# Down-projections of a two-layer decoder trunk: seven pairs of chunks by seven products in place of eight

## The chip, the cores and the metric

The kernel runs on one core of one Trainium2 chip, in one launch. The time is the device time of an execution in microseconds (us). The engines are PE (matmuls; PEld is its loading of the stationary operand), DVE, ACT, POOL, and SP, which here issues nearly all transfers (DMA). Tiles live in SBUF, and matmul results in PSUM, which has eight banks of 128 x 512 fp32.

## What is computed

The reference is a trunk of two layers over a stream of 512 tokens with 1024 features. Layer 0 has dilated window attention, layer 1 forgetting attention, and each is followed by a gated feed-forward network (FFN) with a causal convolution of width 3. The change is in that network, whose hidden width is 2816:

```python
def conv_ffn(xn, w_up, cw, cb, w_down):
    a = xn @ w_up
    ...
    a = sum(ap[:, j:j + T] * cw[j] for j in range(CONV_W)) + cb
    gate, val = jnp.split(a, 2, axis=-1)
    return (jax.nn.gelu(gate, approximate=True) * val) @ w_down
...
    f = conv_ffn(rms_norm(h, g[2]), w_up[l], conv_w[l], conv_b[l], w_down[l])
    h = h + rms_norm(f, g[3])
```

So the down-projection is a product of 512 x 2816 hidden values with a weight of 2816 x 1024, once in each layer.

## The kernel before, in words

**Precision.** Every fp32 operand is split into a high part (a cast to fp32r on ACT) and a low part (the rest, a subtraction on DVE). A product is three matmuls into one bank, high by high, high by low and low by high: `mm3`, lines 236 to 238.

**Weights.** The class `Weights` (line 25 on) holds the list of all weight pieces, 128 x 1024 fp32 or 0.5 MB each, in the order of their use. `load` issues their transfers on SP (line 41), a few pieces ahead; `high` casts a piece on ACT (line 49) and `low` makes the low part on DVE (line 55); `get` hands out the next piece, and `take` gives raw pieces to code that does its own splitting. Raw pieces live in the pool `p4` (9 buffers of 4 KB a partition), split ones in `p8` (17 buffers of 8 KB). A new tile waits for the last use of the tile whose buffer it gets.

**Order.** The program is written out by hand in Python; every engine runs its own instructions in that order, and so does SP with its transfers. A wait on one instruction holds up all that stands behind it on the same engine.

**The FFN** (`ffn`). The hidden width is cut into 22 chunks of 128. For each chunk c, PE multiplies two weight pieces (gate and value) with the transposed input into two banks of 128 features x 512 tokens; ACT and DVE apply the convolution (`taps`, lines 535 to 538), ACT the GELU (line 554), DVE the product of both (line 551), and the result goes to DRAM (`hD`). The chunks in `SEVEN` (6, 8, ..., 20) are done as 2 x 2 blocks in Strassen's way (Winograd's form): seven products of half size (256 wide) in place of eight, with sums of weights made on DVE (`seven_weights`) and sums of the input made once (`sums_in`). While chunk c runs, the steps of `weights(c + 2)` are worked off between its products.

**The down-projection** (`Proj`). For each of the 22 chunks, the hidden values come back from `hD` two chunks at a time (`load_h`, line 516, tile hraw), are split (`prep`, lines 523 and 524, tile hs), and are the stationary operand, 128 tokens at a time; the weight piece (128 x 1024) is the moving one, in two halves of 512. The four token blocks by two halves take all eight banks (`acc`), each being added to over all chunks. A chunk is 4 x 2 x 3 = 24 matmuls. The first 18 chunks run chunk by chunk; the last four (R = 4) run bank by bank, so that each finished bank can be normed and added to the stream while PE goes on. In chunks 20 and 21 of the up-projections the first two hidden tiles and the first weights of the down-projection are prepared already (`load_h(0)`, `prep(0)`, `prep(1)`, `plain_weights`).

## Time and profile before

| what | value |
|---|---|
| median of 3 runs | 1158.45 us (1158.24 to 1158.78) |
| the profiled execution | 1158.71 us |
| its span, first to last instruction | 1156.9 us |
| mean granted clock of PE | 0.999 |
| PE, DVE, ACT, POOL busy | 99%, 66%, 48%, 11% of the span |
| moved by DMA | 138.90 MB, 120 GB/s in the mean |
| down-projection of layer 0, on PE | from 419.08 us on |

A row of the order of time has start, duration, engine, line, operation, output<-input and shape, then in brackets the idle time before it and what ended that. A row of a group has the count, then busy time and mean duration in ns, then the idle time before such instructions and what ended it. A row of busy time by stretch has the stretch, its length, busy time and number of instructions of PE, PEld, DVE, ACT and POOL, the granted clock, the share of the DMA engines and GB/s. Matmuls are pipelined: the distance of two starts is what one costs, and the duration is longer than that.

### The profile page before, as it was taken

What the parts mean: (1) busy time and instruction counts of PE and PEld (TensorE: products, weight loads), DVE (VectorE), ACT (ScalarE), POOL (GpSimd) and SP (SyncE); (2) the same over time, 40 slices, a digit from 0 to 9 for tenths busy, and PEclk for the clock granted to TensorE, in tenths of its full rate; (3) what the DMA queues carried; (4) which work ended last, traced back from release to release, by engine and by line L of the source; (5) the groups of instructions that cost most, each with busy time, mean ns of one, the idle gap of its engine ahead of it and who ended that gap; (6) DMA issues with size and microseconds to landing.
All of it is one profiled execution on the core that took longest, in us unless ns stands there. A gap on an engine that the chain in (4) does not pass through costs nothing.

```text
span 1156.9 us, 16648 instructions
## 1 busy us (share of the span) xinstructions
PE 1142.1 (99%) x6474; PEld 977.5 (84%) x6474; DVE 767.1 (66%) x1227; ACT 554.9 (48%) x956; POOL 131.5 (11%) x191
## 2 busy tenths in 40 slices
PE   9999999999999999999999999999999999999997
PEld 6888889888998888888778888789888998888886
DVE  6433488888878766306564788758788888867204
ACT  5444565444445545305452677755454444445202
POOL 2722003000000000000000565502100000000000
PEclk9999999999999999999999999999999999999999
DMA  8131064334344449203304344274334434539001
GB/s 295 56 111 37 2 173 123 101 110 143 112 127 140 154 158 375 75 1 78 89 1 129 101 118 126 77 203 128 101 92 129 145 105 143 169 124 379 1 1 73
DMA packets 147176, 138.90 MB, mean 120 GB/s; under 512 B 6809, under 2 KB 120969, under 8 KB 147098
## 3 DMA queue, kind: packets, MB, share of 16 engines
q1 hardware_dynamic: 145818, 133.64, 36.7%
q0 software_dynamic: 1280, 4.20, 1.6%
q8 instruction: 51, 0.84, 0.3%
q14 instruction: 27, 0.22, 0.1%
HBM read 119.94 MB, written 13.68 MB: 116 GB/s over the span
## 4 chain that ended last, share of the span: by engine, by line
PE 90%; DVE 4%; ACT 3%; issue 2%; DVEq 0%; ACTq 0%
PE up L236 12%; PE up L237 12%; PE up L238 12%; PE acc L236 9%; PE acc L238 9%; PE acc L237 9%; PE v_ps L236 2%; PE v_ps L238 2%; PE v_ps L237 2%; PE qk_ps L237 2%; PE qk_ps L236 2%; PE qk_ps L238 2%; PE first L238 1%; PE first L236 1%; PE first L237 1%
## 5 line engine op out<-in xcount | busy, mean ns | idle before, releaser
L55 DVE TENSOR_TENSOR w<-wraw,w 128x1024 fp32r<-128x1024 f32 x150 | 189.6, 1279 | 119.2 <-ACT w L49 117.4
L49 ACT CAST w<-wraw 128x1024 fp32r<-128x1024 f32 x150 | 154.2, 1049 | 81.4 <-PE acc L238 56.0
L236 PE MATMUL acc<-w,hs 128*128 128x512 f32 (+1 forms) x356 | 137.9, 387 | 1.1 <-DVE mix L283 1.1
L238 PE MATMUL acc<-w,hs 128*128 128x512 f32 (+1 forms) x356 | 137.6, 387 | 0.0
L237 PE MATMUL acc<-w,hs 128*128 128x512 f32 (+1 forms) x356 | 137.6, 387 | 0.0
L535 ACT ACTIVATE bb<-up,conv 128x512 f32<-128x512 f32 x80 | 60.4, 775 | 149.3 <-DVE up L686 90.9
L236 PE MATMUL up<-xch,w 128*128 128x512 f32 (+1 forms) x288 | 102.2, 355 | 1.7 <-DVE csum L671 1.7
L236 PE MATMUL up<-xbh,w 128*128 128x512 f32 (+1 forms) x288 | 102.1, 355 | 1.7 <-DVE csum L671 1.7
L237 PE MATMUL up<-xcl,w 128*128 128x512 f32 (+1 forms) x288 | 102.0, 354 | 0.0
L237 PE MATMUL up<-xbl,w 128*128 128x512 f32 (+1 forms) x288 | 102.0, 354 | 0.0
L238 PE MATMUL up<-xch,w 128*128 128x512 f32 (+1 forms) x288 | 101.8, 354 | 0.0
L238 PE MATMUL up<-xbh,w 128*128 128x512 f32 (+1 forms) x288 | 101.8, 354 | 0.0
L236 PEld LDWEIGHTS acc<-w,hs 128*128 128x128 f32 x356 | 66.8, 188 | 14.8 <-DVE mix L283 1.3
L237 PEld LDWEIGHTS acc<-w,hs 128*128 128x128 f32 x356 | 66.8, 188 | 13.6
L238 PEld LDWEIGHTS acc<-w,hs 128*128 128x128 f32 x356 | 66.8, 188 | 13.5
L236 PE MATMUL up<-xsh,w 128*128 128x256 f32 x256 | 72.4, 283 | 0.0
L237 PE MATMUL up<-xsl,w 128*128 128x256 f32 x256 | 72.4, 283 | 0.0
L238 PE MATMUL up<-xsh,w 128*128 128x256 f32 x256 | 72.4, 283 | 0.0
L536 DVE SCALAR_TENSOR_TENSOR bb<-up,conv,bb 128x511 f32<-128x511 f32 x80 | 59.4, 743 | 7.2 <-ACT bb L535 7.2
L276 ACT ACTIVATE junk<-acc 128x512 bf16<-128x512 f32 (+1 forms) x33 | 19.2, 582 | 92.4 <-PE acc L238 92.1
L236 PEld LDWEIGHTS up<-xbh,w 128*128 128x128 f32 x288 | 54.4, 189 | 9.5 <-ACT w L49 1.8
L236 PEld LDWEIGHTS up<-xch,w 128*128 128x128 f32 x288 | 54.4, 189 | 9.5 <-ACT w L49 1.8
(273 smaller groups left out, 2662.4 us busy)
## 6 DMA issues: line engine op xcount, KB each, us to landing
wraw<-in_w_up_dram SPq DMA_DIRECT2D x88, 512.0 KB
wraw<-in_w_down_dram SPq DMA_DIRECT2D x44, 512.0 KB
hD<-hc SPq DMA_DIRECT2D x44, 256.0 KB
hraw<-hD SPq DMA_DIRECT2D x22, 512.0 KB
wraw<-in_w_kvf_dram SPq DMA_DIRECT2D x16, 512.0 KB
wraw<-in_w_qkv_a_dram SPq DMA_DIRECT2D x16, 256.0 KB
wraw<-in_w_q_b_dram SPq DMA_DIRECT2D x8, 512.0 KB
ck<-cd SPq DMA_DIRECT2D x8, 512.0 KB
```

What stands on the lines that cost most here:

```text
L49: self.nc.scalar.copy(pair[:, 0], raw)
L55: self.nc.vector.tensor_tensor(pair[:, 1], raw, pair[:, 0].bitcast(F32), ALU.subtract)
L236: pe.matmul(o, ah, bh, start=first, stop=False, skip_group_check=shared)
L237: pe.matmul(o, ah, bl, start=False, stop=False, skip_group_check=shared)
L238: pe.matmul(o, al, bh, start=False, stop=last, skip_group_check=shared)
L276: act.activation(junk[:, :s.stop - s.start], o, AF.Square, scale=1.0 / 32, accum_out=ss[:, n % 2:n % 2 + 1])
L535: act.activation(bb[:, s, :], ps, AF.Identity, bias=cp[:, 3, ch:ch + 1], scale=cp[:, 2, ch:ch + 1])
L536: dve.scalar_tensor_tensor(bb[:, s, 1:], ps[:, :T - 1], cp[:, 1, ch:ch + 1], bb[:, s, 1:], ALU.mult, ALU.add)
```

## The change

Chunks 0 to 13 of the down-projection become seven pairs. A pair is a 2 x 2 block product: the halves of the tokens (256 each) by its two chunks, times its two chunks by the halves of the output (512 each). It is done with seven products of halves and sums in place of eight. The seven pairs are added up product by product, so the sums that belong to the outputs have to be undone in the banks only once, for all pairs together.

- First pass: for each pair, `pair_one` makes sums and differences of the two weight pieces and of the two hidden chunks and splits three tiles; `mul_one` runs four of the seven products, into four banks for each of two block pairs bp (token blocks bp and bp + 2).
- `combine_one`: four additions on DVE and two copies on ACT turn the four banks of a block pair, in place, into the starts of the four outputs.
- Second pass: for each pair, `pair_two` takes the second chunk's weights again (loaded a second time), and the remaining operands, and `mul_two` runs the other three products, added straight into the banks.
- The order of the weight pieces follows: 0 to 13, then 1, 3, ..., 13 again, then 14 to 21.
- Chunks 14 to 21 run in `Proj` as before, which now begins at chunk 14 with the banks that it is given.
- `SEVEN` ends at 18, so chunk 20 of the up-projection is done with whole products. During chunks 20 and 21 `pair_one(0)` and `pair_one(1)` are worked off, in place of the splitting of whole weights and of `prep`.

```diff
+SEVEN = range(6, 19, 2)
+ND = 7
...
-        add_rows(w_down[l], NF)
+        add_rows(w_down[l], [*range(2 * ND), *range(1, 2 * ND, 2), *range(2 * ND, NF)])
...
-        def __init__(self, KC, R, get_act):
+        def __init__(self, KC, R, get_act, begin=0, banks=None):
...
-    SEVEN = range(6, NF - 1, 2)
...
         def weights(c):
+            if c >= NF:
+                return pair_one(c - NF)
             return seven_weights(c) if c in SEVEN else plain_weights()
+        acts, keep, one, two = {}, {}, {}, {}
+        Q = [slice(i * 256, i * 256 + 256) for i in range(4)]
+        H = slice(0, 512), slice(512, 1024)
+
+        def pair_load(j):
+            if j < ND:
+                acts[j] = t8([128, 2, 1024], name="dact")[:, 0]
+                keep[j] = t8([128, 2, 1024], name="dkeep")
+                sp.dma_start(acts[j][:, H[0]], hD[2 * j])
+                sp.dma_start(keep[j][:, 0, H[0]], hD[2 * j + 1])
+
+        def pair_one(j):
+            pair_load(j + 1)
+            r0, r1 = W.take(2)
+            a, k, t = acts.pop(j), keep[j][:, 0], keep[j][:, 1]
+            wa, wb, ac = (t8([128, 2, 1024], F32R, name="w") for _ in range(3))
+            dve.tensor_tensor(t[:, H[1]], r1[:, H[1]], r0[:, H[1]], ALU.subtract)
+            dve.tensor_tensor(r0[:, H[1]], r0[:, H[1]], r0[:, H[0]], ALU.subtract)
+            act.copy(wa[:, 0], r0)
+            yield
+            dve.tensor_tensor(t[:, H[0]], r1[:, H[1]], r0[:, H[1]], ALU.subtract)
+            act.copy(wb[:, 0], t)
+            dve.tensor_tensor(a[:, Q[3]], a[:, Q[0]], a[:, Q[1]], ALU.subtract)
+            dve.tensor_tensor(a[:, Q[1]], a[:, Q[1]], k[:, Q[1]], ALU.add)
+            yield
+            dve.tensor_tensor(a[:, Q[2]], a[:, Q[1]], a[:, Q[0]], ALU.subtract)
+            act.copy(ac[:, 0], a)
+            dve.tensor_tensor(wa[:, 1], r0, wa[:, 0].bitcast(F32), ALU.subtract)
+            yield
+            dve.tensor_tensor(wb[:, 1], t, wb[:, 0].bitcast(F32), ALU.subtract)
+            yield
+            dve.tensor_tensor(ac[:, 1], a, ac[:, 0].bitcast(F32), ALU.subtract)
+            dve.tensor_tensor(k[:, Q[2]], k[:, Q[0]], a[:, Q[2]], ALU.subtract)
+            one[j] = ac, wa, wb
+
+        def pair_two(j):
+            r1, = W.take(1)
+            k, t = keep[j][:, 0], keep[j][:, 1, H[0]]
+            w, ac = (t8([128, 2, 1024], F32R, name="w") for _ in range(2))
+            t4p = t4([128, 2, 512], F32R, name="wsum")
+            act.copy(w[:, 0], r1)
+            dve.tensor_tensor(t, r1[:, H[0]], t, ALU.subtract)
+            act.copy(t4p[:, 0], t)
+            act.copy(ac[:, 0, 0:768], k[:, 0:768])
+            dve.tensor_tensor(w[:, 1], r1, w[:, 0].bitcast(F32), ALU.subtract)
+            dve.tensor_tensor(t4p[:, 1], t, t4p[:, 0].bitcast(F32), ALU.subtract)
+            dve.tensor_tensor(ac[:, 1, 0:768], k[:, 0:768], ac[:, 0, 0:768].bitcast(F32), ALU.subtract)
+            two[j] = ac, w, t4p
...
+        def mul_one(j, bp):
+            ac, wa, wb = one[j]
+            for key, q, w, c in (((bp, 0), 0, wa, H[0]), ((bp, 1), 2, wb, H[0]),
+                                 ((bp + 2, 0), 3, wb, H[1]), ((bp + 2, 1), 1, wa, H[1])):
+                if j == 0:
+                    db[key] = bank([128, 512], name="acc")
+                product_of(db[key], ac, q, w, c, bp, j == 0)
+
+        def combine_one(bp):
+            a, b, c, d = db[bp, 0], db[bp, 1], db[bp + 2, 0], db[bp + 2, 1]
+            p1, u, u3 = (t2([128, 512], name="dsum") for _ in range(3))
+            act.copy(p1, a)
+            dve.tensor_tensor(u, b, p1, ALU.add)
+            dve.tensor_tensor(c, c, u, ALU.add)
+            act.copy(u3, c)
+            dve.tensor_tensor(b, d, u, ALU.add)
+            dve.tensor_tensor(d, d, u3, ALU.add)
+
+        def mul_two(j, bp):
+            ac, w, t4p = two[j]
+            product_of(db[bp, 0], ac, 0, w, H[0], bp, False)
+            product_of(db[bp + 2, 0], ac, 1, t4p, H[0], bp, False)
+            product_of(db[bp, 1], ac, 2, w, H[1], bp, False)
...
+        def down_pairs():
+            for j in range(ND - 2):
+                run(pair_one(j + 2))
+                for bp in range(2):
+                    mul_one(j, bp)
+                del one[j]
+            pair_two(0)
+            for bp in range(2):
+                for j in (ND - 2, ND - 1):
+                    mul_one(j, bp)
+                combine_one(bp)
+                if bp == 0:
+                    pair_two(1)
+            one.clear()
+            for j in range(ND):
+                if j + 2 < ND:
+                    pair_two(j + 2)
+                if j == 0:
+                    continue
+                if j == ND - 4:
+                    load_h(ND)
+                if j >= ND - 2:
+                    W.n_get = W.n_split if j == ND - 2 else W.n_get
+                    W.split(W.n_get + 2 * (j - ND + 3))
+                if j == ND - 1:
+                    prep(ND)
+                for bp in range(2):
+                    for i in ((0, 1) if j == 1 else (j,)):
+                        mul_two(i, bp)
...
         for c in range(2, NF):
-            if c == NF - 2:
-                load_h(0)
-            if c == NF - 1:
-                prep(0)
-                prep(1)
+            if c == NF - 3:
+                pair_load(0)
...
+        down_pairs()
         W.ahead = 4
-        Proj(NF, 4, get_act).finish(nxt, ahead)
+        Proj(NF, 4, get_act, 2 * ND, db).finish(nxt, ahead)
```

`product_of(o, ac, q, w, c, bp, first)` is one `mm3` with quarter q, block bp of the activations and half c of the weights; `run` works off all steps of a generator. `Proj` with begin > 0 takes the banks it is given and starts its loop over chunks there.

More of the change, by code (lines that the diff above doesn't have):

```diff
@@ L129, in trunk_kernel, with add_rows @@
         add(lambda raw, s=s: [(raw.rearrange("p (k c) -> p k c", k=2), cols(wqkv, 2 * s, 2, 1792, 512))])
-    def add_rows(w, n):
-        for kc in range(n):
+    def add_rows(w, chunks):
+        for kc in chunks:
             add(lambda raw, kc=kc: [(raw, w[kc * 128:(kc + 1) * 128, :])])
@@ L141, in add_ffn @@
             add_cols(w_up[l], DFF + c * 128)
-        add_rows(w_down[l], NF)
-    add_rows(w_o_a[0], 6)
+        add_rows(w_down[l], [*range(2 * ND), *range(1, 2 * ND, 2), *range(2 * ND, NF)])
+    add_rows(w_o_a[0], range(6))
     add_ffn(0)
@@ L156, in trunk_kernel @@
         add_cols(w_q_b[0], c * 128)
-    add_rows(w_o_b[0], 8)
+    add_rows(w_o_b[0], range(8))
     add_ffn(1)
@@ L342, in step @@
             mm3(self.banks[b, hf][:, part], ah[:, s], al[:, s], w[0][:, c], w[1][:, c],
-                kc == 0, kc == self.KC - 1, part.start > 0)
+                kc == 0, kc == self.KC - 1, part.start > 0 or self.begin > 0)
         def both(self, kc, b):
@@ L353, in finish @@
             if hook is None:
-                for kc in range(n):
+                for kc in range(self.begin, n):
                     for b in range(NB):
@@ new lines, in run @@
+        def run(steps):
+            for _ in steps:
+                pass
+        def down_pairs():
[27 more added lines that the diff above has]
+                        mul_two(i, bp)
+            two.clear()
```

13 lines of the change are left out of this document (9 added, 4 removed).

## The prediction

> **What bounds the kernel now.** I read the page first, then busy time by stretch, then the order of time on PE, DVE, ACT and SP around the end of the up-projections and the start of the down-projections. The page:
>
> ```profile
> span 1156.9 us, 16648 instructions
> ...
> PE 1142.1 (99%) x6474; PEld 977.5 (84%) x6474; DVE 767.1 (66%) x1227; ACT 554.9 (48%) x956; POOL 131.5 (11%) x191
> ...
> PE 90%; DVE 4%; ACT 3%; issue 2%; DVEq 0%; ACTq 0%
> ```
>
> PE is the bound, and the chain of waits runs through it for 90% of the span. Busy time by stretch (PE, PEld, DVE, ACT, POOL) for the first and the second part of layer 0's down-projection shows what else is near it:
>
> ```profile
> 418.90:455.00 36.10, 36.10 (x161) 29.90 (x160) 28.89 (x27) 22.30 (x23) 0.00 (x0) 1.00 0.86 327
> 455.00:495.00 40.00, 40.00 (x178) 33.12 (x177) 12.34 (x11) 10.23 (x10) 0.00 (x0) 1.00 0.35 112
> ```
>
> PE never stops there. DVE is 80% busy for 36 us, because it runs ahead, and 31% after. So matmuls taken away count in full only while DVE, which has to prepare the halves and sums, keeps ahead. PE's durations overlap; what counts is the distance of starts. Ten matmuls lie between these two rows of PE's order of time:
>
> ```profile
> 493.65 0.39 PE L238 MATMUL acc<-w,hs 128*128 128x512 f32 x1
> ...
> 495.92 0.39 PE L236 MATMUL acc<-w,hs 128*128 128x512 f32 x1
> ```
>
> That is 0.227 us for a matmul 512 wide, not the 0.39 of its row.
>
> **What goes from PE.** Per layer, 14 chunks x 4 token blocks x 2 halves x 3 matmuls = 336 become 7 pairs x 2 block pairs x 7 products x 3 = 294: 42 fewer, 9.5 us, or 76.3 us down to 66.7. The same 512-wide form stays. Both layers: 19 us if all is hidden.
>
> **What comes to PE in the up-projections.** SEVEN ends at chunk 18, so chunk 20 goes back to whole products. Sixty steps of 256-wide matmuls lie between the first two rows, and the other two show PE's longest wait in the FFNs:
>
> ```profile
> 376.62 0.28 PE L236 MATMUL up<-xsh,w 128*128 128x256 f32 x1
> ...
> 383.82 0.40 PE L236 MATMUL up<-xbh,w 128*128 128x512 f32 x1
> ...
> 400.38 0.28 PE L238 MATMUL up<-xsh,w 128*128 128x256 f32 x1
> 402.32 0.36 PE L236 MATMUL up<-xbh,w 128*128 128x256 f32 x1 [1.66 <-DVE csum L671]
> ```
>
> A 256-wide matmul takes 0.12. Chunk 20's 84 of them (10.1) become 48 of 512 (10.9): 0.8 us more per layer. The wait of 1.66 comes from whole weights being split inside a chunk of seven products; it moves from chunk 20 to chunk 18, whose steps now split chunk 20's whole weights, and so neither goes nor grows.
>
> **What comes to DVE, and where it is on the path.** pair_one has ten DVE instructions: three sums of 512, four of 256, three low parts of 1024. Four must wait for the one before on DVE. Starts of like instructions in DVE's order of time:
>
> ```profile
> 380.05 0.68 DVE L600 TENSOR_TENSOR wsum<-wsum,wraw 128x512 f32<-128x512 f32 x1
> 380.77 0.69 DVE L602 TENSOR_TENSOR wsum<-wraw,wsum 128x512 f32<-128x512 f32 x1
> 381.85 1.22 DVE L604 TENSOR_TENSOR w<-wsum,w 128x1024 fp32r<-128x1024 f32 x1 [0.39 <-ACT w L601]
> ...
> 384.37 1.22 DVE L607 TENSOR_TENSOR w<-wraw,w 128x1024 fp32r<-128x1024 f32 x1
> 385.50 0.43 DVE L684 TENSOR_TENSOR up<-up,csum 128x256 f32<-128x256 f32 x1
> 385.83 1.22 DVE L610 TENSOR_TENSOR w<-wsum,w 128x1024 fp32r<-128x1024 f32 x1
> ...
> 406.91 0.43 DVE L679 TENSOR_TENSOR up<-up,csum 128x256 f32<-128x256 f32 x1 [3.27 <-PE up L238]
> 407.38 0.43 DVE L684 TENSOR_TENSOR up<-up,csum 128x256 f32<-128x256 f32 x1
> ...
> 421.86 0.74 DVE L536 SCALAR_TENSOR_TENSOR bb<-up,conv,bb 128x511 f32<-128x511 f32 x1
> 422.63 0.75 DVE L538 SCALAR_TENSOR_TENSOR bb<-up,conv,bb 128x510 f32<-128x510 f32 x1
> 423.47 0.69 DVE L551 TENSOR_TENSOR hc<-bb 128x512 f32<-128x512 f32 x1
> 424.08 1.22 DVE L55 TENSOR_TENSOR w<-wraw,w 128x1024 fp32r<-128x1024 f32 x1
> ```
>
> 512 takes 0.61 (L551), 0.72 when the next needs its result (L600 to L602); 256 takes 0.33, or 0.47 (L679 to L684); 1024 takes 1.13 (L607). In pair_one's order: 0.72 + 0.72 + 0.61 + 0.47 + 0.47 + 0.33 + 3 x 1.13 + 0.33 = **7.0 us a pair**. PE needs 24 x 0.227 = **5.4 us a pair**. So in the first pass DVE sets the time. ACT does not; its three casts cost 1.05 each and each has 0.8 us or more of DVE work ahead of the low part that needs it:
>
> ```profile
> L49 ACT CAST w<-wraw 128x1024 fp32r<-128x1024 f32 x32 | 33.1, 1048 | 39.3 <-PE acc L238 34.0 <-DMA wraw<-in_w_down_dram 5.3
> ...
> L608 ACT CAST w<-wraw 128x512 fp32r<-128x512 f32 x3 | 1.8, 616 | 0.0
> ```
>
> Pairs 0 and 1 are prepared in chunks 20 and 21: 7.0 + 3.5 us of taps and product against PE's 10.9 there, so they are ready. The other five start after the last taps. Call T the first matmul of the down-projection (419.08):
>
> ```profile
> 418.85 0.39 PE L238 MATMUL up<-xbh,w 128*128 128x512 f32 x1
> 419.08 0.39 PE L236 MATMUL acc<-w,hs 128*128 128x512 f32 x1
> ```
>
> ```profile
> 1030.07 0.78 ACT L535 ACTIVATE bb<-up,conv 128x512 f32<-128x512 f32 x1 [0.15 <-PE up L238]
> ```
>
> The last up matmul ends at T + 0.2, ACT's 0.78 brings T + 1.0, the two taps and the product (421.86 to 424.08) 2.2 more: pair 2 starts on DVE at T + 3.25. Pair 6 starts four pairs later at T + 31.3; its last low part starts 5.6 later and takes 1.2: T + 38.1. PE's third matmul of pair 6 waits for that. 34 matmuls of the first pass stand behind it (7.7): the pass ends at T + 45.9, against T + 38.1 without waits.
>
> **The second pass** is 126 matmuls, 28.6 us. I cost its preparation and the combining at nothing; PE hides them. From T + 38.1 DVE has left: 0.3 of pair 6, pair_two for pairs 0, 1 and 2 (0.6 + 1.13 + 0.6 + about 0.9 for 768 elements = 3.2 each), and two combinings (four sums of 512 with dependences and a copy on ACT between, 2.9 each): 15.7, done at T + 53.8. PE first needs pair 2's at T + 45.9 + 36 x 0.227 = T + 54.1, two matmuls later for the low part. It is the tightest cover, 0.8 us; after it DVE gains 0.9 a pair (3.2 against 4.1). Bank sums in PSUM have no 512-wide tensor-tensor row here; from 0.61 to the taps' 0.77, I take 0.61 plus dependences, the upper end costing 1.3 of which 0.8 is covered. The combining waits hold up only pair_two behind them on DVE and ACT. So the change ends at T + 45.9 + 28.6 = T + 74.5, against T + 76.3: 1.8 us less, not 9.5.
>
> **Transfers.** Pass one loads 1.5 MB a pair, and behind hD's last write (the product at T + 3.25) on SP wait pair 3's activations and weights. Before, the like sequence on SP, and when its last transfer reached ACT in layer 0:
>
> ```profile
> 424.19 0.32 SPq L704 DMA_DIRECT2D hD<-hc  x1
> 424.56 0.43 SPq L41 DMA_DIRECT2D wraw<-in_w_down_dram  x1
> 425.39 0.37 SPq L516 DMA_DIRECT2D hraw<-hD  x1
> 425.87 0.88 SPq L41 DMA_DIRECT2D wraw<-in_w_down_dram  x2
> ```
>
> ```profile
> 433.76 1.05 ACT L49 CAST w<-wraw 128x1024 fp32r<-128x1024 f32 x1 [0.25 <-DMA wraw<-in_w_down_dram]
> 435.09 1.06 ACT L523 CAST hs<-hraw 128x1024 fp32r<-128x1024 f32 x1 [0.28 <-DMA hraw<-hD]
> ```
>
> 2.25 MB took 9.5 us, at 1.3 per 0.5 MB in the steady state. Pair 3's 1.75 MB takes 8.2: T + 11.5, and DVE wants it at T + 10.3: 1.2 us late. In layer 1 the same five transfers took 8.1:
>
> ```profile
> 1034.98 0.32 SPq L704 DMA_DIRECT2D hD<-hc  x1
> ```
>
> ```profile
> 1043.07 1.05 ACT L49 CAST w<-wraw 128x1024 fp32r<-128x1024 f32 x1 [0.24 <-DMA wraw<-in_w_down_dram]
> ```
>
> There it is in time. From nothing to 1.2 in each layer, I take 0.7 in all. Later pairs need 3.9 us of transfer in 7. The second load of the odd chunks (0.5 MB per 4.1 us) is hidden too, and of hraw's 11 loads and casts a layer 4 are left, the other seven being pair_load's 14 of half the size, counted above. Chunks 14 to 21 run as before, and their weights are split by T + 72, before PE gets there.
>
> **Sum.** Per layer 1.8 - 0.8 = 1.0 gained, two layers 2.0, less 0.7: 1.3. The profiled execution took 1158.71 with a span of 1156.9; the median of the runs shown is 0.26 lower, 1158.45. 1158.71 - 1.3 - 0.26 = **1157.2 us**, with 1155 to 1159.5 as this case's own range: within 0.2% (2.3 us, about what a measurement of this kernel can tell from no change).
>
> **Rivals.** *Dependences are free.* If DVE starts a dependent instruction like any other, a pair costs 6.5, 2.4 us less per layer: 1152.4. The rows L600 to L602 and L679 to L684 speak against it, since both show 0.11 to 0.14 more. The Trainium skill ("VectorE: DVE Perf Modes", The DRAIN you can't avoid) says that a semaphore between chained DVE instructions costs nothing extra; by that rule this rival would hold, and the trace disagrees. Chance 0.15. *All hidden*: 19 less 1.6, 1141; DVE's 7.0 against 5.4 speaks against it. 0.03.
>
> *The clock.* PE leaves block pair 0 of pair 5 at T + 33.4 (low part T + 31.1, ten more matmuls) and gets pair 6's low part at T + 38.1; two matmuls that need only high parts fall into this gap at T + 35.8, so the longest wait is 2.4. PE's slow matmuls are seen once, at the start:
>
> ```profile
> 9.86 0.63 PE L237 MATMUL qk_ps<-w,xah 128*128 128x512 f32 x1
> 10.29 0.63 PE L238 MATMUL qk_ps<-w,xal 128*128 128x512 f32 x1
> 10.71 0.50 PE L236 MATMUL qk_ps<-w,xah 128*128 128x512 f32 x1
> ```
>
> Steps of 0.42 in place of 0.227. After the 1.66 us wait none follows (402.32). Slow again for some 3.2 us (7.5 to 10.7) would cost 1.5 per layer: 1160.2. The Trainium skill ("TensorE: Matmul & The Clock Gate", Part 1) has PE fall to half rate after about 3.4 us idle; no wait in this trace is as long. Chance 0.08.
>
> *The hand-overs between DVE and ACT show* (slower). L604 waited 0.39 for its cast. The covers of 0.8 speak against it in pair_one; transfers or ACT's order could use them up. From 0.36 a pair the change is slower than before by over 0.2%; with two such waits a pair, 0.78 x 5 = 3.9 per layer, it is 1165. Or DVE falls behind in the second pass in the same way. Chance 0.23.
>
> **How the numbers follow.** My case has 0.51: 0.18 of it below 1156.1 (layer 0's transfer in time, the chains a little shorter), 0.33 within 0.2%. Faster: 0.18 + 0.15 + 0.03 = 0.36. Same: 0.33 + 0.05 of the clock's 0.08 = 0.38. Slower: 0.23 + 0.03 = 0.26. The range goes from 1152.2 (dependences free) to 1164.5 (just under two hand-over waits a pair), leaving about 0.1 beyond either end.
>
> **What would show it.** On DVE, five times ten instructions 7.0 apart in the first pass, with the three low parts not waiting for ACT; PE waiting 1.6 us before pairs 4 and 5 and twice about 2 before pair 6, each time for the low part of the activations; no PE wait in the second pass; the wait for csum once, at chunk 18. I am wrong if the pairs stand under 6.6 or over 7.4 apart, if pair 3 waits long for its weights, if PE waits at the first products of the second pass, or if the matmuls after the waits stand 0.42 apart.

## The result and the profile after

The changed kernel takes **1165.95 us** (median of 6 runs, 1164.44 to 1166.12) against 1158.76 for the kernel before (6 runs on the same chip): the ratio is 1.0059, with a 95% interval of 1.0046 to 1.0072. It is slower by 7.2 us; 1157.2 was forecast, and 1164.5 was the upper end of the range. The profiled execution took 1164.44, which is 5.73 more than that of before. In the other executions the mean granted clock was 0.991 to 0.994; this one had 0.994.

The page of the changed kernel (the lines that were shown of before):

```profile
span 1162.7 us, 16610 instructions
...
PE 1130.9 (97%) x6318; PEld 960.9 (83%) x6318; DVE 856.5 (74%) x1375; ACT 586.6 (50%) x1000; POOL 131.7 (11%) x191
...
PE 85%; DVE 8%; issue 3%; ACT 3%; DMA 1%; SPq 0%; DVEq 0%; ACTq 0%
```

PE has 156 matmuls fewer and is busy 11 us less, yet the span is 6 us longer. In the chain of waits PE has 5 points of the span less, and DVE 4 more. What PE waited for in layer 0's down-projection (from the waits of PE: total us, times, longest):

```profile
PE acc L243 <- DVE w L671: 5.7, 4, 1.6
PE acc L241 <- ACT w L666: 2.2, 1, 2.2
```

L671 is the low part of the activations in `pair_one`, as forecast; L666 is the cast that makes their high part. The lines of the changed kernel stand a few further down than those of the kernel before: L236 to L238 are L241 to L243 now. DVE's order of time, the first instruction (L656) of pairs 2 to 5, and the last low part of pair 6 (L671):

```profile
422.81 0.69 DVE L656 TENSOR_TENSOR dkeep<-wraw 128x512 f32<-128x512 f32 x1
...
431.29 0.69 DVE L656 TENSOR_TENSOR dkeep<-wraw 128x512 f32<-128x512 f32 x1 [1.34 <-DMA wraw<-in_w_down_dram]
...
438.34 0.68 DVE L656 TENSOR_TENSOR dkeep<-wraw 128x512 f32<-128x512 f32 x1
...
445.39 0.69 DVE L656 TENSOR_TENSOR dkeep<-wraw 128x512 f32<-128x512 f32 x1
...
458.03 1.22 DVE L671 TENSOR_TENSOR w<-dact,w 128x1024 fp32r<-128x1024 f32 x1
```

The pairs stand 7.05 apart (forecast 7.0), and DVE never idles between them except before pair 3, where the weights come 1.34 late. In layer 1 the same wait is there too:

```profile
1044.61 0.69 DVE L656 TENSOR_TENSOR dkeep<-wraw 128x512 f32<-128x512 f32 x1 [1.28 <-DMA wraw<-in_w_down_dram]
```

PE's order of time at pair 6, where it waits twice with two matmuls between:

```profile
457.01 0.50 PE L241 MATMUL acc<-w 128*128 128x512 f32 x1 [2.20 <-ACT w L666]
457.35 0.40 PE L242 MATMUL acc<-w 128*128 128x512 f32 x1
459.30 0.79 PE L243 MATMUL acc<-w 128*128 128x512 f32 x1 [1.56 <-DVE w L671]
459.89 0.63 PE L241 MATMUL acc<-w 128*128 128x512 f32 x1
460.32 0.63 PE L242 MATMUL acc<-w 128*128 128x512 f32 x1
...
462.45 0.48 PE L241 MATMUL acc<-w 128*128 128x512 f32 x1
```

From 459.30 to 462.45 the matmuls stand 0.43 apart, and last 0.63: they run at half clock. Busy time of PE by stretch (length, busy time, number of matmuls that lie in it at least in part, granted clock, share of the DMA engines, GB/s) shows how long, for both layers; the borders are put where the clock changes:

```profile
435.35:438.76 3.41, 1.82 (x8) 1.00 1.03 403
438.76:442.17 3.41, 3.41 (x17) 1.00 1.03 397
455.82:459.24 3.42, 0.73 (x2) 1.00 0.39 135
459.24:462.65 3.41, 3.35 (x8) 0.50 0.08 24
462.65:466.06 3.41, 3.41 (x17) 1.00 0.38 135
1066.81:1070.22 3.41, 1.33 (x6) 1.00 0.36 124
1070.22:1073.64 3.42, 2.23 (x4) 0.50 0.08 30
1073.64:1077.05 3.41, 3.41 (x10) 0.50 0.42 89
```

The clock falls for one stretch of 3.41 us in layer 0 and for two in layer 1. Each time the 3.41 us ahead of the fall hold few matmuls: two, and six, where 15 start at full rate. In layer 1 the fall comes at 1070.22, ahead of the second wait: the stretch ahead of it holds the wait for the cast alone, and the second wait (1.07 there) lies in the first slow stretch, which is followed by another. The eight of the stretch from 435.35 on, with a wait of 1.59 in it, were not followed by a fall.

**The account of the profiled execution.** T is again the first matmul of the down-projection, at 419.55 in layer 0 and 1032.93 in layer 1.

| us per layer | forecast | layer 0 | layer 1 |
|---|---|---|---|
| T later than before (layer 1: beyond the 2.02 from layer 0) | +0.8 | +0.47 | +1.04 |
| third matmul of pair 6, at T + | 38.1 | 39.75 | 39.70 |
| from there to the second pass (34 matmuls) | 7.7 | 9.40 | 9.90 |
| second pass (126 matmuls) | 28.6 | 28.56 | 28.56 |
| first matmul of chunk 14, at T + (before: 76.2) | 74.5 | 77.7 | 78.2 |

So in layer 0 the 9.5 us of matmuls saved meet 9.4 us of waiting in the first pass (49.15 long, where 168 matmuls take 38.1, less the clock's part), 1.7 of half clock and 0.5 in the up-projection: some 2.0 slower. Layer 1 adds 3.0, so the last matmul of the kernel ends 5.06 later (start at 1155.99 against 1150.93). DVE's last instruction comes 5.06 later too (1157.39 against 1152.33), so the other 0.7 of the 5.73 lies behind it, where the output is stored; its cause was not followed up.

### The profile page after: what moved, and what is told of

It reads as the page before. It is cut to its first block, busy times and chain, and to the rows that moved or that the text cites. A ratio compares the mean times of both kernels' runs of the same rounds, so it can differ in the third digit from the quotient of the medians.

```text
span 1162.7 us, 16610 instructions
## 1 busy us (share of the span) xinstructions
PE 1130.9 (97%) x6318; PEld 960.9 (83%) x6318; DVE 856.5 (74%) x1375; ACT 586.6 (50%) x1000; POOL 131.7 (11%) x191
## 4 chain that ended last, share of the span: by engine, by line
PE 85%; DVE 8%; issue 3%; ACT 3%; DMA 1%; SPq 0%; DVEq 0%; ACTq 0%
PE up L241 12%; PE up L242 12%; PE up L243 12%; PE acc L243 7%; PE acc L241 7%; PE acc L242 7%; PE v_ps L241 2%; PE v_ps L243 2%; PE v_ps L242 2%; PE qk_ps L242 2%; PE qk_ps L241 2%; PE qk_ps L243 2%; PE first L241 1%; PE first L243 1%; PE first L242 1%
## 5 line engine op out<-in xcount | busy, mean ns | idle before, releaser
L59 DVE TENSOR_TENSOR w<-wraw,w 128x1024 fp32r<-128x1024 f32 x126 | 159.6, 1291 | 61.1 <-ACT w L53 60.7
L53 ACT CAST w<-wraw 128x1024 fp32r<-128x1024 f32 x126 | 128.6, 1048 | 17.4 <-DMA wraw<-in_w_up_dram 7.0
L241 PE MATMUL up<-xch,w 128*128 128x512 f32 (+1 forms) x292 | 104.9, 359 | 1.7 <-DVE csum L799 1.7
L241 PE MATMUL up<-xbh,w 128*128 128x512 f32 (+1 forms) x292 | 104.9, 359 | 1.7 <-DVE csum L799 1.7
L243 PE MATMUL up<-xch,w 128*128 128x512 f32 (+1 forms) x292 | 104.7, 358 | 0.0
L243 PE MATMUL up<-xbh,w 128*128 128x512 f32 (+1 forms) x292 | 104.7, 358 | 0.0
L243 PE MATMUL acc<-w 128*128 128x512 f32 x168 | 68.1, 405 | 11.0 <-DVE w L671 11.0
L241 PE MATMUL acc<-w 128*128 128x512 f32 x168 | 67.4, 401 | 4.4 <-ACT w L666 4.4
L242 PE MATMUL acc<-w 128*128 128x512 f32 x168 | 66.8, 398 | 0.0
L241 PEld LDWEIGHTS up<-xch,w 128*128 128x128 f32 x292 | 55.1, 189 | 10.1 <-ACT w L53 1.8
L241 PEld LDWEIGHTS up<-xbh,w 128*128 128x128 f32 x292 | 55.1, 189 | 10.1 <-ACT w L53 1.8
L243 PE MATMUL up<-xsh,w 128*128 128x256 f32 x224 | 63.4, 283 | 0.0
L241 PE MATMUL up<-xsh,w 128*128 128x256 f32 x224 | 63.4, 283 | 0.0
L242 PE MATMUL up<-xsl,w 128*128 128x256 f32 x224 | 63.4, 283 | 0.0
L546 DVE SCALAR_TENSOR_TENSOR bb<-up,conv,bb 128x510 f32<-128x510 f32 x80 | 59.9, 749 | 2.8
L242 PEld LDWEIGHTS up<-xcl,w 128*128 128x128 f32 x292 | 55.1, 189 | 8.1
L243 PEld LDWEIGHTS up<-xbh,w 128*128 128x128 f32 x292 | 55.1, 189 | 8.2
L242 PEld LDWEIGHTS up<-xbl,w 128*128 128x128 f32 x292 | 55.1, 189 | 8.1
```

The lines of the kernel that those rows point to most:

```text
L53: self.nc.scalar.copy(pair[:, 0], raw)
L59: self.nc.vector.tensor_tensor(pair[:, 1], raw, pair[:, 0].bitcast(F32), ALU.subtract)
L241: pe.matmul(o, ah, bh, start=first, stop=False, skip_group_check=shared)
L242: pe.matmul(o, ah, bl, start=False, stop=False, skip_group_check=shared)
L243: pe.matmul(o, al, bh, start=False, stop=last, skip_group_check=shared)
L546: dve.scalar_tensor_tensor(bb[:, s, 2:], ps[:, :T - 2], cp[:, 0, ch:ch + 1], bb[:, s, 2:], ALU.mult, ALU.add)
```

## The experiments

Two theories stood against each other for the miss. *The clock*: the half clock that follows PE's two waits before pair 6 costs 1.7 and 2.2 us; it is lost time because the second pass is bound by PE. *DVE alone*: the chain on DVE, with the late weights, sets the end, and the slow matmuls hide behind it or come from something else. Each ratio is to the kernel before, run beside it on the same chip.

| run | edit | us, median | ratio (95% interval) | third matmul of pair 6, T + (layer 0, 1) | second pass, T + (layer 0, 1) |
|---|---|---|---|---|---|
| | the changed kernel | 1165.95 | 1.0059 (1.0046 to 1.0072) | 39.75, 39.70 | 49.15, 49.60 |
| e1 | PE's gaps filled | 1161.53 | 1.0025 (1.0016 to 1.0034) | 40.31, 40.02 | 48.15, 47.86 |
| e2 | weights loaded earlier | 1162.22 | 1.0029 (1.0017 to 1.0040) | 38.31, 38.33 | 48.61, 47.68 |
| e3 | two instructions on POOL | 1180.65 | 1.0185 (1.0171 to 1.0199) | 47.55, 47.20 | 58.22, 57.26 |
| e4 | before, with SEVEN to 18 | 1160.41 | 1.0014 (1.0005 to 1.0023) | | |
| e5 | one low part left out on DVE | 1154.37 | 0.9964 (0.9950 to 0.9977) | 36.44, 36.10 | 44.26, 43.93 |
| e6 | DVE's order | 1161.26 | 1.0022 (1.0013 to 1.0030) | 37.61, 37.54 | 47.05, 47.00 |
| e7 | e2 and e6 | 1157.71 | 0.9992 (0.9983 to 1.0001) | 35.83, 35.85 | 46.33, 46.49 |
| e8 | e7, gap filled, low parts in another order | 1159.44 | 1.0006 (0.9997 to 1.0015) | 38.36, 38.37 | 45.52, 45.53 |
| e9 | e7, gaps filled | 1152.99 | 0.9951 (0.9938 to 0.9963) | 35.84, 35.84 | 43.68, 43.65 |
| e10 | e9, two products moved | 1151.65 | 0.9942 (0.9929 to 0.9956) | 35.84, 35.84 | 42.31, 42.30 |
| e11 | e10, pair 2 begun earlier | 1152.53 | 0.9948 (0.9935 to 0.9960) | 36.33, 36.33 | 42.81, 42.80 |
| e12 | e10 without the zero-adding matmuls | 1152.32 | 0.9942 (0.9929 to 0.9956) | 35.84, 35.84 | 42.32, 42.32 |

### e1: PE's gaps filled

```diff
+        def fill(n):
+            for _ in range(n):
+                pe.matmul(db[1, 0][0:64], zr, zr[:, None, :].to_broadcast([128, 8, 64]), start=False, stop=False, skip_group_check=True)
...
         def mul_one(j, bp):
             ac, wa, wb = one[j]
+            if (j, bp) == (ND - 1, 0):
+                s = slice(0, 128)
+                fill(9)
+                pe.matmul(db[0, 0], ac[:, 0, s], wa[:, 0, H[0]], ...)
+                pe.matmul(db[0, 0], ac[:, 0, s], wa[:, 1, H[0]], ...)
+                fill(6)
+                pe.matmul(db[0, 0], ac[:, 1, s], wa[:, 0, H[0]], ...)
...
+                if (j, key) == (ND - 1, (0, 0)):
+                    continue
```

`zr` holds zeros, so the fill changes no sum.

> Edit: the changed kernel, with matmuls that add zero to a bank put into PE's two gaps before pair 6: nine ahead of pair 6's first matmul and six ahead of its third. DVE's work is untouched. Theory (the clock): PE's low activity before pair 6, two matmuls in about 4.5 us, brings the granted clock to one half for one or two stretches of 3.4 us per layer; the matmuls after it stand 0.43 instead of 0.227 apart, which costs 1.6 us in layer 0 and 2.4 us in layer 1 in the profiled execution. With the gaps filled the clock stays at 1.00, no matmul of pair 6 stands 0.42 from the next, and the time falls by 4 to 5.5 us, to about 1161. Rival (DVE is the bound in the second pass as well): the clock stays up, but PE then waits for pair_two or for the combining, and the time falls by 1.5 us at most. Rival (the slow matmuls come from the banks that DVE and ACT combine beside them, not from idle time): the matmuls stay 0.42 apart, no gain.

Measured: 1161.53, 4.4 less than the changed kernel in the medians and 2.2 less in the profiled executions (1162.23 against 1164.44). PE's order of time at the same place:

```profile
458.72 1.48 PE L702 MATMUL acc<-zr 128*64 128x512 bf16 x6
460.35 0.50 PE L712 MATMUL acc<-w 128*128 128x512 f32 x1
460.68 0.39 PE L244 MATMUL acc<-w 128*128 128x512 f32 x1
460.91 0.39 PE L245 MATMUL acc<-w 128*128 128x512 f32 x1
```

The matmuls behind the gap stand 0.23 apart, though DVE's low part came no earlier (T + 40.3). The banks are combined as before, so they are not the cause, and the second pass had no shadow for the slow matmuls to hide in: it starts 1.0 and 1.7 us earlier. The theory of the clock held. In layer 1 of this run the clock fell elsewhere, once, behind pair 3's wait:

```profile
1048.00:1051.40 3.40, 1.75 (x8) 1.00 1.02 394
1051.40:1054.80 3.40, 3.40 (x8) 0.50 0.99 349
```

Eight matmuls in a stretch, which in the changed kernel was enough (435.35), was not enough here; that is on the edge.

### e2: the weights loaded earlier

```diff
             pair_load(j + 1)
+            W.ahead_dma = 4 if 1 <= j < ND - 1 else 2
```

> Edit: the changed kernel with the weights of the pairs loaded two pairs ahead instead of one (ahead_dma 4 while pairs 1 to 5 are prepared), so that pair 3's weights are issued ahead of the last writes to hD. Theory (transfers): DVE's wait of 1.3 us before pair 3 goes in both layers, everything behind it in the first pass comes 1.3 earlier; the clock still falls before pair 6, since the gaps there are as long as before. 2.6 us less, about 1163.3. Rival (the first pass's end is not set by that chain): no change. If the clock's fall depends on where in its stretches the gap lies, the time may move by a further 1 us either way.

Measured: 1162.22, 3.7 less. Pair 3 follows pair 2 on DVE with no wait (its first row in DVE's order of time, with no bracket behind it):

```profile
430.04 0.69 DVE L657 TENSOR_TENSOR dkeep<-wraw 128x512 f32<-128x512 f32 x1
```

The third matmul of pair 6 comes at T + 38.3, close to the forecast's T + 38.1. So the late weights cost 1.4 in each layer. The clock still fell behind pair 6 in both layers, as expected; the second pass is at T + 48.6 and T + 47.7 by how many stretches it stayed down.

### e3: two of DVE's instructions on POOL

```diff
-            dve.tensor_tensor(wb[:, 1], t, wb[:, 0].bitcast(F32), ALU.subtract)
+            pool.tensor_tensor(wb[:, 1], t, wb[:, 0].bitcast(F32), ALU.subtract)
...
-            dve.tensor_tensor(k[:, Q[2]], k[:, Q[0]], a[:, Q[2]], ALU.subtract)
+            pool.tensor_tensor(k[:, Q[2]], k[:, Q[0]], a[:, Q[2]], ALU.subtract)
```

> Edit: the changed kernel with two of pair_one's ten DVE instructions on POOL, which is idle there: the low part of the weight sums (1024 wide) and the sum that only the second pass needs (256 wide). POOL takes 5.12 us for 2048 elements in the kernel before, so some 2.6 and 0.7 here. Theory (DVE's 7.05 us a pair against PE's 5.44 set the first pass): DVE's pair falls to 5.6; pair 3 still waits for its weights, pair 6's last low part lands about T + 33 instead of T + 39.7, PE's waits shrink to one or two of some 3 us before pair 6, and the time falls by 6 per layer, or 8 if the clock stays up: about 1150 to 1154. Rival (DVE and POOL slow each other): DVE's 1024-wide low parts take over 1.5 us instead of 1.22 and the pair stays near 7; no gain or slower. Rival (POOL is late with the low part): PE waits for POOL instead of DVE, same time.

Measured: 1180.65, 14.7 more. The theory's number failed, and the first rival was right. DVE's order of time in this run, and then POOL's:

```profile
437.83 1.22 DVE L667 TENSOR_TENSOR w<-wraw,w 128x1024 fp32r<-128x1024 f32 x1
439.02 3.32 DVE L671 TENSOR_TENSOR w<-dact,w 128x1024 fp32r<-128x1024 f32 x1
442.26 1.21 DVE L656 TENSOR_TENSOR dkeep<-wraw 128x512 f32<-128x512 f32 x1
```

```profile
438.08 3.17 POOL L669 TENSOR_TENSOR w<-dkeep,w 128x1024 fp32r<-128x1024 f32 x1 [4.80 <-DMA dkeep<-hD]
441.22 1.71 POOL L672 TENSOR_TENSOR dkeep<-dkeep,dact 128x256 f32<-128x256 f32 x1
```

The same instruction on DVE took 1.22 in the changed kernel (458.03) and takes 3.32 where it starts while POOL runs one with two operands. It ends 1.09 behind POOL's, so it did next to nothing until POOL was done. L667, which had started 0.25 ahead of POOL's, still took 1.22. The 512-wide sum beside POOL's next takes 1.21 instead of 0.69 (L656 in the changed kernel). What POOL takes over, DVE loses beside it, at POOL's slower rate. The waits also bring the clock down more often: this profile has eight stretches of half clock in the two first passes, against three, so the 14.7 are not POOL's alone.

### e4: SEVEN to 18 alone, in the kernel before

```diff
-    SEVEN = range(6, NF - 1, 2)
+    SEVEN = range(6, 19, 2)
```

> Edit: the kernel before with SEVEN ending at 18, so chunk 20 of both up-projections is done with whole products; nothing else of the change. The prediction priced this at 0.8 us per layer; in the two profiles the down-projection starts 0.47 later in layer 0 and 1.04 later, beyond what came before, in layer 1. Theory: 1.5 us in all, about 1160.3. Rival: the splitting of whole weights in chunk 18 adds a wait there, or takes one away: under 0.5 or over 2.5.

Measured: 1160.41 against 1158.69 for the kernel before, 1.7 more. The term was 1.6.

### e5: one low part left out on DVE

```diff
-            dve.tensor_tensor(wb[:, 1], t, wb[:, 0].bitcast(F32), ALU.subtract)
+            act.copy(wb[:, 1], t)
```

> Edit: the changed kernel in which the low part of the weight sums in pair_one is left out: ACT writes a second cast of the sums in its place, so the output isn't the reference's; the time is what is looked at. DVE loses one 1024-wide instruction of ten, ACT gains a cast. Theory (DVE alone sets the first pass): DVE's pair falls from 7.05 to 5.9 us; pair 3 still starts at T + 11.7, when its weights are there; pair 6's last low part lands at T + 35.2 instead of T + 39.7, so 4.5 less per layer, 9 in all, and up to 13 if the clock stays up: 1153 to 1157. Rival (something other than DVE's count of work, such as transfers or hand-overs from ACT, holds the pairs 7 apart): under 3 us less.

Measured: 1154.37, 11.6 less. Two of the pairs' first rows in DVE's order of time:

```profile
444.23 0.69 DVE L656 TENSOR_TENSOR dkeep<-wraw 128x512 f32<-128x512 f32 x1
...
450.27 0.68 DVE L656 TENSOR_TENSOR dkeep<-wraw 128x512 f32<-128x512 f32 x1
```

They stand 6.04 apart, pair 3 waited 3.0 for its weights in layer 0, and the third matmul of pair 6 came at T + 36.4 and T + 36.1. DVE's count of work does set the first pass. In this profile the granted clock stayed at 1.00 around pair 6 in both layers. The second wait had shrunk to 0.53, behind a first one of 2.29. Where the clock's stretches lie mattered too: counted back from the fall at the run's end (1150.69), a border stands at 454.37, inside the first wait, and the stretch ahead of it is half busy:

```profile
450.96:454.37 3.41, 1.68 (x8) 1.00 0.29 74
```

### e6: DVE's instructions in another order

```diff
             dve.tensor_tensor(t[:, H[1]], r1[:, H[1]], r0[:, H[1]], ALU.subtract)
+            dve.tensor_tensor(a[:, Q[3]], a[:, Q[0]], a[:, Q[1]], ALU.subtract)
             dve.tensor_tensor(r0[:, H[1]], r0[:, H[1]], r0[:, H[0]], ALU.subtract)
             act.copy(wa[:, 0], r0)
             yield
+            dve.tensor_tensor(a[:, Q[1]], a[:, Q[1]], k[:, Q[1]], ALU.add)
             dve.tensor_tensor(t[:, H[0]], r1[:, H[1]], r0[:, H[1]], ALU.subtract)
             act.copy(wb[:, 0], t)
-            dve.tensor_tensor(a[:, Q[3]], a[:, Q[0]], a[:, Q[1]], ALU.subtract)
-            dve.tensor_tensor(a[:, Q[1]], a[:, Q[1]], k[:, Q[1]], ALU.add)
             yield
```

> Edit: the changed kernel with pair_one's ten DVE instructions in another order, so that none follows directly on the one whose result it reads; the work is the same. Theory (a dependent DVE instruction starts 0.11 to 0.14 later, as the prediction took it): four such places go, a pair takes 6.55 instead of 7.05, pair 6's last low part comes 1.9 earlier per layer: 3.8 us less, about 1162, with 2 us either way for where the clock falls. Rival (the dependences are free and the rows' differences come from the shapes and operands): 7.05 stays, no change.

Measured: 1161.26, 4.7 less. The same ten instructions, by the first row of two pairs in DVE's order of time:

```profile
438.85 0.69 DVE L656 TENSOR_TENSOR dkeep<-wraw 128x512 f32<-128x512 f32 x1
...
445.40 0.69 DVE L656 TENSOR_TENSOR dkeep<-wraw 128x512 f32<-128x512 f32 x1
```

6.55 apart in place of 7.05: the four dependent starts cost 0.12 each, as the prediction took them, and it is the order that cost it, not the work.

### e7: early loads and the new order

The edit is those of e2 and e6 together.

> Edit: the new order of e6 and the early loads of e2 together. Theory (both terms sit on the same chain on DVE and add up): pair 3 starts with no wait, pairs stand 6.55 apart, pair 6's last low part lands at T + 35.8 instead of T + 39.7: 3.9 less per layer, 7.8 in all, about 1158 if the clock falls as often as in the changed kernel. Rival (the transfers, 3.9 us of the 6.55 per pair, become late when the pairs are closer): pairs 4 to 6 wait for weights, and it stays near e2's 1162.

Measured: 1157.71, as expected, and the third matmul of pair 6 stands at T + 35.83 where T + 35.8 was expected. The two terms add up. The transfers are in time for the pairs at 6.55. The time can't be told from that of the kernel before. The clock still falls, for two stretches in each layer of this profile (and for one more at 731.09, between the two down-projections), as PE's order of time shows:

```profile
454.07 0.50 PE L241 MATMUL acc<-w 128*128 128x512 f32 x1 [2.33 <-ACT w L667]
...
455.73 0.79 PE L243 MATMUL acc<-w 128*128 128x512 f32 x1 [0.88 <-DVE w L672]
456.32 0.63 PE L241 MATMUL acc<-w 128*128 128x512 f32 x1
```

### e8: a fill, two products moved, and another order of the low parts

```diff
-            dve.tensor_tensor(wb[:, 1], t, wb[:, 0].bitcast(F32), ALU.subtract)
-            yield
             dve.tensor_tensor(ac[:, 1], a, ac[:, 0].bitcast(F32), ALU.subtract)
+            yield
+            dve.tensor_tensor(wb[:, 1], t, wb[:, 0].bitcast(F32), ALU.subtract)
...
+            mul_one(ND - 2, 0)
+            mul_one(ND - 2, 1, slice(0, 2))
+            fill(6)
+            mul_one(ND - 1, 0)
...
+            mul_one(ND - 2, 1, slice(2, 4))
+            mul_one(ND - 1, 1)
```

> Edit: e7, and PE's gaps filled: two of pair 5's four products of block pair 1 go ahead of pair 6, then six matmuls that add zero; the low part of the activations is made ahead of that of the weight sums. Theory: the clock stays at 1.00 before pair 6 (1.6 to 2.4 us less per layer than e7), and the two moved products (1.36 us a layer) fill a wait: 4 to 6 less than e7, about 1152 to 1154, faster than the kernel before. Rival (DVE is so late in the second pass that what is gained ahead of it is lost there): PE waits for pair_two or for the combining, 2 to 3 less than e7. Rival (the clock falls in an earlier gap instead): no less than e7.

Measured: 1159.44, 1.7 more than e7. The last rival has this direction, but not this mechanism: the granted clock stayed at 1.00 in both passes. The reordered low part was a mistake: DVE now reaches it before the cast that it needs is done. The waits of DVE in layer 0 (total us, times, longest):

```profile
DVE w L673 <- ACT w L670: 3.2, 5, 0.7
```

DVE waits 0.64 in each of the five pairs, which now stand 7.29 apart (L660 at 430.29 and 437.58) in place of 6.55. PE also waits in the second pass here (0.47 for L691). This is the rival "hand-overs between DVE and ACT" of the prediction, made here by an edit; the changed kernel does not have it.

### e9: e7 with the gaps filled

```diff
+            mul_one(ND - 2, 0)
+            fill(9)
+            mul_one(ND - 1, 0)
             ...
         def product_of(o, ac, q, w, c, bp, first, gap=0):
             ...
+            fill(gap)
```

`gap` is 3 for the first product of pair 6 and 0 elsewhere.

> Edit: e7 (early loads, DVE order without dependent neighbours) with zero-adding matmuls in the two gaps before pair 6, nine and three, as in e1. DVE's order and the order of the products are e7's. Theory (the clock): e7's profile has two stretches of half clock in each layer's gap before pair 6; they go, and with them 2 to 2.5 us a layer: about 1153.5. Rival (DVE is the bound behind the gap, and the slow matmuls hide in its shadow, as e8's waits in the second pass suggest): PE waits for pair_two or the combining and it stays at 1156 or more.

Measured: 1152.99, 4.7 less than e7. PE's order of time:

```profile
453.97 0.50 PE L703 MATMUL acc<-w 128*128 128x512 f32 x1 [0.23 <-ACT w L670]
...
454.64 0.83 PE L699 MATMUL acc<-zr 128*64 128x512 bf16 x3
455.64 0.50 PE L706 MATMUL acc<-w 128*128 128x512 f32 x1 [0.16 <-DVE w L675]
455.97 0.39 PE L703 MATMUL acc<-w 128*128 128x512 f32 x1
```

DVE delivers at the same point as in e7 (T + 35.84 against T + 35.83), and the second pass starts 2.7 and 2.8 us earlier. Apart from the zeros, only the clock differs. This is the cleanest pair of runs on it. (The profiled executions, 1158.93 and 1153.53, are 5.4 apart; that of e7 was the slowest of its eleven.)

### e10: two products moved into the gap

```diff
             mul_one(ND - 2, 0)
-            fill(9)
+            mul_one(ND - 2, 1, slice(0, 2))
+            fill(4)
             mul_one(ND - 1, 0)
...
-            mul_one(ND - 2, 1)
+            mul_one(ND - 2, 1, slice(2, 4))
```

> Edit: e9 with two of pair 5's four products of block pair 1 put ahead of pair 6 (then four zero-adding matmuls instead of nine); unlike e8, the low parts on DVE keep e7's order. Theory: the two products (6 matmuls, 1.36 us) run where PE would wait; the second pass begins 1.36 us earlier in each layer and DVE's cover of some 0.8 us ahead of pair_two's results is used up, so 0.8 of it is gained a layer: 1.6 less than e9. Rival (no cover is left): PE waits as much longer in the second pass, no less than e9.

Measured: 1151.65, 1.3 less than e9 (1.6 expected), and 0.58% less than the kernel before: this is the fastest of all. The second pass starts 1.4 earlier in each layer, and half of that is lost again behind a wait that is new there (waits of PE in layer 0):

```profile
PE acc L706 <- DVE w L691: 0.4, 1, 0.4
```

L691 is the low part of `pair_two`'s activations, the prediction's tightest cover.

### e11: pair 2 begun ahead of the last taps

```diff
+        begun = pair_one(2)
+        next(begun)
         post(*before)
...
+                run(begun if j == 0 else pair_one(j + 2))
```

> Edit: e10 with the first step of pair 2's preparation (three DVE sums, 1.5 us) ahead of the last chunk's taps, in place of an idle 0.75 us in which DVE waits for ACT. Theory (DVE's chain sets the first pass's end): everything on DVE behind the taps comes 0.75 earlier, 1.5 less in all than e10. Rival (the taps, now 0.8 later, hold up the banks that pair 0's last products need): PE waits there, no less than e10.

Measured: 1152.53, 0.9 more than e10; the theory failed, and not by the banks: PE has no new wait in the first pass. DVE's order of time, and then ACT's:

```profile
419.38 0.69 DVE L562 TENSOR_TENSOR hc<-bb 128x512 f32<-128x512 f32 x1
421.31 0.75 DVE L547 SCALAR_TENSOR_TENSOR bb<-up,conv,bb 128x511 f32<-128x511 f32 x1 [1.24 <-ACT bb L546]
```

```profile
419.54 1.05 ACT L663 CAST w<-wraw 128x1024 fp32r<-128x1024 f32 x1 [3.64 <-issue]
420.50 1.44 ACT L546 ACTIVATE bb<-up,conv 128x512 f32<-128x512 f32 x2
```

The idle time on DVE did not fill; it moved. The step that was put first holds a cast on ACT (L663) as well as the three sums. That cast now stands ahead of the convolution's instructions (L546) on ACT and waits for DVE's sum, so L546 of the first bank, at 415.89 in e10, comes at 420.50. DVE then waits 1.24 for ACT instead of 0.75, and pair 2's remaining work comes 0.4 later. The sums alone, without the cast, were not tried.

### e12: without the zero-adding matmuls

```diff
             mul_one(ND - 2, 1, slice(0, 2))
-            fill(4)
...
-                product_of(db[key], ac, q, w, c, bp, j == 0, 3 if (j, key) == (ND - 1, (0, 0)) else 0)
+                product_of(db[key], ac, q, w, c, bp, j == 0)
```

> Edit: e10 without its zero-adding matmuls; only the two real products stand in the gap before pair 6. PE then waits about 1.1 us ahead of pair 6's first matmul and 0.9 ahead of its third, with two matmuls between. Theory (the clock goes by how busy PE was in a fixed stretch of 3.41 us: in the profiles so far stretches with matmuls in under a third of them were followed by half clock, and those with more than 0.42 were not): here the worst stretch has two waits of 2.0 us together, 0.41 busy, on the edge; mostly the clock stays up and the time is e10's, 1151.7, up to 1153.5 where it falls once. Rival (any two waits so close bring the clock down): half clock in both layers, 1155 to 1156.

Measured: 1152.32, ratio 0.9942 like e10's. PE's waits in the two passes of layer 0, and its busy time by stretch around the waits at pair 6. The first stretch is put where it holds both waits; the other two have the clock's own borders, counted back in steps of 3.413 from the fall at the run's end (1146.79):

```profile
PE acc L706 <- DVE w L675: 2.1, 3, 0.9
PE acc L703 <- ACT w L670: 1.0, 1, 1.0
```

```profile
452.40:455.80 3.40, 1.50 (x7) 1.00 0.42 154
450.48:453.89 3.41, 2.62 (x12) 1.00 0.23 79
453.89:457.30 3.41, 2.30 (x9) 1.00 0.20 74
```

The clock does not fall. Two waits of 0.98 and 0.93 with two matmuls between leave the clock alone, where 2.33 and 0.88 brought it down (e7), so two waits close together are not enough. This profile does not try the edge that was expected, though: a border parts the two waits, and the clock's own stretches are 0.77 and 0.67 busy (in layer 1 as well), not 0.41. The other four executions, whose borders are not on record, all lie within 0.5 us of this one, less than the 1.7 that one fall cost, which speaks against a fall in any of them. Nor does the expectation's count hold for all profiles before, by the busy time of these rows: in e1 the clock fell behind a stretch that was 0.51 busy. And real products do for the gap what zeros do.

## Why the prediction was wrong, point by point

**Right.** A matmul's distance of 0.227 and the 42 fewer per layer; DVE as the bound of the first pass, at 7.05 a pair (forecast 7.0); pair 2's start at T + 3.26 (3.25); PE's waits before pairs 4 and 5 for the low part of the activations, 1.32 and 1.27 (forecast 1.6), and two before pair 6, 2.20 and 1.56 (forecast 2.4 and about 2), though the first of them is for ACT's cast and not for the low part; the second pass at 28.56 without a wait (28.6); the chunk that goes back to whole products, 1.7 in all (1.6; e4). The dependent starts on DVE cost what the rows of before said (e6), so the rival *dependences are free* is out: reordering took 0.5 off each pair. The Trainium skill ("VectorE: DVE Perf Modes", The DRAIN you can't avoid) says of a chain of copies that the semaphore between them costs nothing extra; here a chain of dependent sums took longer than the same sums in another order. Whether the semaphore or the wait for the result takes the 0.12, no run here separates. The hand-overs between DVE and ACT, on which most of the chance of a slower kernel was put, show in neither layer: in the first pass of both, DVE waits for nothing but pair 3's weights.

**Mis-sized: the transfers.** The prediction worked out T + 11.5 for pair 3's weights in layer 0, took them to be in time in layer 1 and charged little ("From nothing to 1.2 in each layer, I take 0.7 in all"). Pair 3 started at T + 11.74 and T + 11.68, 1.34 and 1.28 late: 2.6 in all, and e2 gave back 3.7 of the time. The faster transfers that layer 1 showed before were no measure for the new sequence.

**Wrong: the step in "The clock".** The prediction had the mechanism, its place and nearly its price, but gave it a chance of 0.08 and put it at nothing in its sum, because "two matmuls that need only high parts fall into this gap ..., so the longest wait is 2.4" and the 1.66 wait of before had left no slow matmuls. It judged the clock by the longest single wait. What counted was how little PE did in a fixed stretch of 3.41 us: 0.73 us with parts of both waits in layer 0, and 1.33 with the wait of 2.20 alone in layer 1. In place of its 1.5 us per layer, 1.7 and 2.2 were measured in the changed kernel, and 2.7 and 2.8 between e7 and e9; e1 and e9, which fill the gaps and change nothing else, gave 4.4 and 4.7 us in the medians.

The Trainium skill ("TensorE: Matmul & The Clock Gate", Part 1) gives both halves of this: a rule that no gap of PE should be longer than about 3.4 us, and a sentence that the window is free-running. The prediction took the first. The traces agree with the second: the two falls of the changed kernel begin 610.98 us apart (459.24 and 1070.22), 179 stretches of 3.413. They don't agree with the first as a limit: the longest wait was 2.2 in the changed kernel and 1.58 in e1, and the clock fell behind both.

**The sum.** Against the forecast's -1.3 the profiled execution came out at +5.7. Of the 7.0 between, the clock is 3.9, the transfers 1.9 (2.6 less 0.7), the rest of DVE's chain 0.6 (pair 6's low part 0.3 later per layer than 7.0 a pair gives with the transfers in), and 0.7 the end of the run, less 0.1 by which the whole-product chunk cost less than its 1.6. The median of the six runs is 1.5 above the profiled one, with a granted clock down to 0.991; that more stretches at half clock make this up is argued from those clocks, not shown.

**Where the 19 us of saved matmuls went.** A pair that DVE sets costs 7.05 in the first pass and 18 x 0.227 = 4.1 in the second: 11.1, where two chunks cost 10.9 before. Such a pair gains nothing; only those prepared ahead do. With the order of e6 it is 6.55 + 4.1 = 10.6, and so e7 breaks even, and e9 and e10, with the clock kept, are 0.49% and 0.58% faster than before.

## What to carry to other kernels

When fewer matmuls leave PE waiting for another engine, price the clock with the waits: add up PE's idle time over any 3.4 us, across the few matmuls that stand between two waits, and fill such a gap with products that are ready (e10, e12) before counting the saving. Where one engine sets the distance of the steps, put its independent instructions between the dependent ones and load its inputs a step earlier first; both cost nothing here and gave 8 us together (e7). And before work is moved to an idle engine, ask what the two share (e3).

## What the runs showed of the hardware

- The granted clock went to 0.50 in stretches of 3.41 us or twice that, whose borders lie whole multiples of 3.413 apart over the span. In the first passes of the changed kernel it fell behind stretches with PE busy for 0.73 and 1.33 us, and in e1 behind one of 1.75 (1048.00); behind 1.82 it did not (435.35). But it also stayed up behind 1.68 in e5 (450.96) and behind 1.53 in e3 (1077.52 to 1080.93, counted back from the fall at 1087.75). So the busy time of these rows does not settle the bound, which lies near half of the stretch; the rest stays open.
- Where a wait lies among these stretches counts: the wait of 2.29 in e5, parted by a border, was not followed by a fall, and the one of 2.20 in layer 1 of the changed kernel, inside one stretch but for its last 0.12 us, was.
- Matmuls of zeros in bf16 with 64 columns keep the clock up as products do (e1, e9).
- A DVE instruction with two operands from SBUF, 1024 wide in fp32, took 1.22 in the changed kernel and 3.32 where it started beside one of POOL's that took 3.17 (e3): it ended 1.09 behind POOL's. One that had started 0.25 ahead of POOL's was not slowed. The Trainium skill ("GPSIMD Engine Reference", 8. Key points) names a contention of the two for DVE instructions with two SBUF inputs; the traces agree.
